# Halvings of modulation sums further apart, and a norm spread moved behind the last head's values

## The chip, the cores and the metric

The kernel runs on one core of one Trainium2 chip. The metric is device time in microseconds (us), as the median of several executions. Beside it there is one profiled execution, whose trace gives the start and length of every instruction on the engines: PE (TensorE, the matrix products), DVE (VectorE), ACT (ScalarE), POOL (GpSimd) and the queue SP that issues most transfers. POOL computes a little here and also issues transfers of its own.

## The reference

One decoder layer on 512 tokens of width 1024, in fp32. Two token mixers run side by side, a gated MLP with a short convolution follows, and everything is modulated by six vectors computed from a condition `c`:

```python
cs = jax.nn.silu(c)
mod = cs @ w_ada[l] + b_ada[l]
shift1, scale1, gate1, shift2, scale2, gate2 = jnp.split(mod, 6, axis=-1)
h = _rmsnorm(x, norm1_g[l]) * (1.0 + scale1) + shift1
proj = h @ w_in[l]
qa, ka, va, qd, kd, vd, ga, gd = jnp.split(proj, points, axis=-1)
out_a = _sliding_window_attention(qa, ka, va, sinks, slopes)      # 8 heads
out_d = _diff_attention(qd, kd, vd, lam, ...)                     # 4 heads, below
merged = sigmoid(ga) * (out_a @ w_branch_swa) + sigmoid(gd) * (out_d @ w_branch_diff)
x = x + gate1 * (merged @ w_out)
h2 = _rmsnorm(x, norm2_g[l]) * (1.0 + scale2) + shift2
x = x + gate2 * _conv_ffn(h2, w_up, conv_w, conv_b, w_down)
```

A differential head takes two causal softmax maps over 64-wide queries and keys, subtracts `lam` times the second from the first, multiplies by 128-wide values, and normalises each token's 128 values by their root mean square (`_rmsnorm(out, subln_g)`). That last norm is what the change touches, together with the sums for `gate1`, `shift2`, `scale2` and `gate2`.

## The kernel before, in words

Every fp32 product is made of three matmuls on a rounded high part and a remainder (`mm3`, lines 129 to 132). The weights arrive in blocks over SP, ACT casts the high part (L126), DVE subtracts for the low part (L127).

The work around the change is the stage of the four differential heads, h = 0 to 3, with four blocks of 128 queries each (n = 0 to 3). TensorE does for each block the scores `sd` (both maps), then, when DVE and ACT have made the softmax and the difference, the transposes `td` (`diff_transpose`), which ACT and DVE evacuate into `aTh` and `aTl` (`evac`, L498 and L499). After the last block of a head come its values: `od` = the transposed maps times the values (`diff_values`). ACT then squares `od` (`sq`) and copies it scaled (`of`).

The norm of a head goes in three closures that `diff_values` leaves behind:

- `stats`: four small matmuls `pss` sum the squares for each token, DVE makes the mean square `ms` (L189), and POOL raises it to the power -1/2 (`rstd_start`, L193);
- `end`: four small DVE operations refine that and multiply in the softmax divisor (`rstd_end`, L201 to L203, and L829): `drs`;
- `turn_norm`: four transposes `rb` (L839) spread `drs` over the partitions, DVE multiplies `of` by it (L841), ACT and DVE split the result into `outdA` and `outdB`, the head's input to the branch product `pB`.

Heads 0 to 2 put these into lists (`beside`) that the main loop empties with `flush` at a fixed block of the next head; head 3 has no next head and uses `after(n, ...)`.

Between these pieces TensorE works off other products, step by step: projections, gates (`pga`, `pgd`) and the branch product of the first mixer (`pA`). `fill(n)` issues n such steps (a step is one `mm3` of 128x512), counts down everything that `after` has put off, and at every eighth step lets the sums of the modulation advance by one step (`ada_rows`).

These sums make four rows of 1024 (`gate1`, `shift2`, `scale2`, `gate2`). DVE multiplies blocks of `w_ada` by `cs` and adds them up in `arow`, 128 partitions by 1024 (L888, L890). The sum over the partitions is done by transfers that POOL issues (`ada_sum`, L898): 64 rows are added onto 64, then 32 onto 32, down to one row, and the last transfer writes it to DRAM (`mod_rows`, L901). Each halving has to wait until the one before it has landed, and POOL, which works in order, stands still meanwhile. `HALVE_LAG` is the number of fills from one halving to the next in the written order.

The readers of `mod_rows`: row 0 becomes `g1b`, by which the output weights are multiplied (L1110, L1118, L1135); rows 1 and 2 are loaded by SP into `m2` (`load_m2`, L1079), turned by TensorE (`turn_m2`, L1083), and scale the second norm; row 3 is read in the MLP. In the trace the tile names have lost their trailing digits: `m2` is `m`, `pm2` is `pm`. `M2_LAG` sets the fills from the end of the attention stage to `load_m2` and to `turn_m2`.

The order of the instructions on TensorE and POOL is the written one (`manual_schedule`); DVE, ACT and SP are ordered by a planner, with priorities (`high_priority`) and with holds (`issue_after`: not before that instruction).

Of the kernel before, what the change touches and what calls it, by code (L numbers as in the profile page):

```python
# [28 lines left out]
ADA_AHEAD = 2  # L29
HP = 100000  # L30
ST = 6
HALVE_LAG = 6
ADA_EVERY = 8
ADA_EASY = 20

ROW_BEHIND = {0: -3, 4: -2}
ADA_START = 4
V_LAG = 13
M2_LAG = (48, 60)
STAT_LAG = 10  # L40
END_LAG = 3
NORM_LAG = 16
# [16 lines left out]
def kernel(  # L59
# [44 lines left out]
    def tbank(name, shape=(P, S)):  # L104
        return bank("t", 2, list(shape), name)

    def vbank(name):
        return bank("v", 1, [P, S], name)
# [16 lines left out]
    def split(hi, lo, src):  # L125
        cast = nc.scalar.copy(hi, src)  # L126
        return cast, nc.vector.tensor_sub(lo, src, hi.bitcast(F32))  # L127

    def mm3(o, lh, ll, rh, rl, start, stop):
        nc.tensor.matmul(o, lh, rh, start=start, stop=False)  # L130
        nc.tensor.matmul(o, lh, rl, start=False, stop=False)  # L131
        nc.tensor.matmul(o, ll, rh, start=False, stop=stop)  # L132
# [53 lines left out]
    def rstd_start(ssq, n, d, wpool, plus=None):  # L186
        ms = wpool.tile([P, n], F32, tag="rs_a", bufs=3, name="ms")
        if plus is None:
            nc.vector.tensor_scalar(ms, ssq, 1.0 / d, EPS, ALU.mult, ALU.add)  # L189
        else:  # L190
            nc.vector.scalar_tensor_tensor(ms, ssq, 1.0 / d, plus, ALU.mult, ALU.add)  # L191
        r0 = wpool.tile([P, n], F32, tag="rs_c", bufs=3, name="r0")
        nc.gpsimd.tensor_tensor(r0, ms, mhalf[:, :n], ALU.pow)  # L193
        return ms, r0

    def rstd_end(dst, ms, r0, n, wpool):
        t = wpool.tile([P, n], F32, tag="rs_b", bufs=3, name="rt")
        if n == 1:
            nc.vector.scalar_tensor_tensor(t, r0, r0, ms, ALU.mult, ALU.mult)
        else:  # L200
            nc.vector.tensor_mul(t, r0, r0)  # L201
            nc.vector.tensor_mul(t, t, ms)
        nc.vector.scalar_tensor_tensor(dst, t, -3.0, r0, ALU.add, ALU.mult)  # L203
# [338 lines left out]
    def prefetch():  # L542
        while units and len(loaded) < 2:
            load, run = units.pop(0)
            loaded.append((load(), run))

    def fill(n):
        for _ in range(n):
            if not current:
                prefetch()  # L550
                if loaded and due[0]:
                    due[0] -= 1
                    wts, run = loaded.pop(0)
                    current.append(run(wts))
                    if tick[0]:
                        prefetch()
            if tick[0] == 7:
                prefetch()
            if current:
                try:  # L560
                    next(current[0])
                except StopIteration:
                    current.clear()
            for e in list(later):
                e[0] -= 1
                if e[0] <= 0:
                    later.remove(e)
                    e[1]()
            tick[0] += 1
            if tick[0] >= ADA_START and tick[0] % ADA_EVERY == 0:  # L570
                next(ada, None)
# [3 lines left out]
    def after(n, fn):  # L575
        later.append([n, fn])

    def flush(*kinds):
        for kind in kinds:
            while beside[kind]:  # L580
                beside[kind].pop(0)()
# [209 lines left out]
    def diff_transpose(s):  # L791
        h, n = divmod(s, NT)
        if n == 0:
            aTs[h] = [ap.tile([P, 1664], F32R, tag=g, bufs=2, name=f"{g}{h}") for g in ("aTh", "aTl")]
        tp = tbank(f"td{h}_{n}")
        for k in range(n + 1):
            nc.tensor.transpose(tp[:, k * P : (k + 1) * P], probs[s][:, k * P : (k + 1) * P], ident)
        hi, lo = (a.rearrange("p (b q) -> p b q", q=P)[:, n : 4 * n + 1 : 3] for a in aTs[h])
        with tc.high_priority(offset=HP):
            settled.append(evac(hi, lo, tp[:, : (n + 1) * P].rearrange("p (k q) -> p k q", q=P)))  # L800

    def diff_values(h):
        t, (aTh, aTl) = heads[h], aTs[h]
        o = vbank(f"od{h}")
        for k in range(NT):
            q0 = k * P
            mm3(
                o[:, q0:], t[:, 4, k * P : (k + 1) * P], t[:, 5, k * P : (k + 1) * P],
                aTh[:, k * AW + q0 : k * AW + 512], aTl[:, k * AW + q0 : k * AW + 512],
                k == 0, k == NT - 1,  # L810
            )
        sq = ap.tile([P, S], F32, tag="tmp", bufs=2, name=f"sq{h}")
        of = ap.tile([P, S], F32, tag="of", bufs=2, name=f"of{h}")
        nc.scalar.activation(sq, o, AF.Square)
        nc.scalar.activation(of, o, AF.Copy, scale=sublnc)

        def stats():
            pss = tbank(f"pss{h}", (P, NT))
            for n in range(NT):
                nc.tensor.matmul(pss[:, n : n + 1], sq[:, n * P : (n + 1) * P], ones[:, 0:1], start=True, stop=True)  # L820
            rs, r0, r2 = (ap.tile([P, NT], F32, tag=t, bufs=2, name=f"{t}{h}") for t in ("drs", "dr0", "dr2"))
            nc.vector.reciprocal(r0, sums[h][:, 0])
            nc.vector.tensor_mul(r2, r0, r0)
            nc.vector.tensor_mul(r2, r2, pss)
            half = rstd_start(r2, NT, P, ap)

            def end():
                rstd_end(rs, *half, NT, ap)
                nc.vector.tensor_mul(rs, rs, r0)  # L829

            if h < 3:
                beside["end"].append(end)
            else:
                after(END_LAG, end)

            def turn_norm():
                rb = tbank(f"rb{h}")
                for n in range(NT):
                    nc.tensor.transpose(rb[:, n * P : (n + 1) * P], rs[:, n : n + 1].to_broadcast([P, P]), ident)  # L839
                with tc.high_priority(offset=HP):  # L840
                    nc.vector.tensor_mul(of, of, rb)  # L841
                split(outd[0][:, h], outd[1][:, h], of)

            if h < 3:
                beside["norm"].append(turn_norm)
            else:
                after(NORM_LAG, turn_norm)

        if h < 3:
            beside["sum"].append(stats)  # L850
        else:
            after(STAT_LAG, stats)
# [42 lines left out]
    def ada_sum(idx, whole):  # L895
        def step(n):
            if n:
                nc.gpsimd.dma_start(whole[0:n], whole[n : 2 * n], accum_op=ALU.add)  # L898
                after(HALVE_LAG, lambda: step(n // 2))
            else:  # L900
                nc.gpsimd.dma_start(mod_rows[idx : idx + 1], whole[0:1].rearrange("o a n -> o (a n)"))  # L901

        after(1, lambda: step(P // 2))
# [98 lines left out]
    for s in range(4 * DIFF_HEADS):  # L1002
        h, n = divmod(s, NT)
        if s in (4, 8):
            due[0] += 3
        elif s == 12:
            due[0] += 4
        ahead = s == 1
        fill(DIFF_FILL[1] - ahead)
        nxt = (s + 1, s + 2) if n % 2 and s < 15 else ()  # L1010
        if nxt:
            diff_scores(*nxt)
        if n == 3:
            with tc.issue_after(maxima[-1].ins):
                flush("end")
        if n == 1:
            diff_transpose(s)
        fill(DIFF_FILL[2] + ahead)
        if n == 2:
            flush("sum")  # L1020
        elif n == 0:
            flush("norm")
        if n != 1:
            diff_transpose(s)
        diff_softmax(*nxt)
        if n == 0 and h:
            diff_values(h - 1)
            fill(DIFF_FILL[3])
    due[0] += 2 * (KT - 4)
    fill(4)  # L1030
    flush("norm")
    diff_values(DIFF_HEADS - 1)
    while due[0] or current:
        fill(1)
    at.close()
# [52 lines left out]

    after(M2_LAG[0], load_m2)
    after(M2_LAG[1], turn_m2)  # L1090

# [880 lines left out]
```

## Time and profile before

| | |
|---|---|
| median of 3 executions | 690.01 us (689.94 to 692.77) |
| the profiled execution | 691.2 us, of which the span from first to last instruction 689.4 us |
| mean granted TensorE clock | 0.994 of full |
| TensorE busy | 677.5 us, 98% of the span |
| DVE, ACT, POOL busy | 563.9, 382.2, 100.1 us |
| halvings on POOL | 28, the first at 135.26, the last at 315.25 us |

A page of the profile lists busy times by engine, then the span in 40 slices with a digit for each engine, then the chain of waits that ended last, then groups of instructions. A row of a timeline has the start, the length, the engine, the line, the operation, its output and inputs, and in brackets how long the engine sat idle before it and what ended that. A row of the chain has start, length and what the time went to. A list of waits has who waited for whom, the total, the number and the longest. A row of the windows has for each engine its busy time and number of instructions, then the granted TensorE clock, the share of the DMA engines and the rate.

### The profile page before, as it was taken

How to read it: one execution, taken by the hardware profiler on the slowest of the kernel's cores; microseconds unless marked ns; L12 is line 12 of the kernel's file. 1: busy time of each engine (PE TensorE's matmuls, PEld its weight loads, DVE VectorE, ACT ScalarE, POOL GpSimd, SP SyncE). 2: the span in 40 equal slices, each digit the busy share in tenths (PEclk: the TensorE clock that was granted, in tenths of full speed). 3: DMA queues.
4: the chain of work that ended last, by engine and by line, in shares of the span. 5: the costliest groups of instructions: out<-in, count | busy, mean ns of one | idle time of the engine just before them, and what ended most of it. 6: DMA issues, size and time to landing. Idle time of an engine off the chain costs nothing.

```text
span 689.4 us, 11101 instructions
## 1 busy us (share of the span) xinstructions
PE 677.5 (98%) x4139; PEld 593.0 (86%) x4139; DVE 563.9 (82%) x1073; ACT 382.2 (55%) x678; POOL 100.1 (15%) x121
## 2 busy tenths in 40 slices
PE   8999999999989999999999999999999999999995
PEld 5887787888878888788899999999999999888885
DVE  5999775988775676793589988888888999979997
ACT  7676674546442323333377656655555666656665
POOL 3000000021012101111030011112110102440300
PEclk9999999999999999999999999999999999999998
DMA  9995412565455687569635788777979647995903
GB/s 306 351 295 180 131 61 76 166 167 157 139 145 160 215 256 201 170 175 327 216 67 119 181 209 191 170 168 216 208 212 220 155 161 182 196 205 144 168 1 122
DMA packets 116934, 123.89 MB, mean 180 GB/s; under 512 B 4983, under 2 KB 93848, under 8 KB 116880
## 3 DMA queue, kind: packets, MB, share of 16 engines
q1 hardware_dynamic: 97038, 95.11, 43.1%
q0 software_dynamic: 19648, 27.79, 23.8%
q8 instruction: 32, 0.52, 0.3%
q10 hardware_dynamic: 194, 0.28, 0.1%
q14 instruction: 22, 0.18, 0.1%
HBM read 118.97 MB, written 2.11 MB: 176 GB/s over the span
## 4 chain that ended last, share of the span: by engine, by line
PE 95%; DMA 2%; DVE 1%; ACT 0%; issue 0%; SPq 0%; POOL 0%; POOLq 0%; ACTq 0%
PE up L1300 32%; PE dc L1916 15%; PE a L393 5%; PE pgd L130 2%; PE pgd L131 2%; PE pgd L132 2%; PE oc L1356 2%; PE oc L1360 2%; PE oc L1357 2%; PE pga L130 2%; PE pga L132 2%; PE pga L131 2%; PE pq L130 1%; PE pw L130 1%; PE sd L137 1%; DMA adaw<-in_w_ada_dram 1%
## 5 line engine op out<-in xcount | busy, mean ns | idle before, releaser
L1300 PE MATMUL up<-t,m_whi 128*128 128x256 f32 x512 | 93.1, 283 | 0.0
L1300 PEld LDWEIGHTS up<-t,m_whi 128*128 128x128 f32 x512 | 79.9, 192 | 0.0
L1300 PE MATMUL up<-t,m_wlo 128*128 128x256 f32 x256 | 72.4, 283 | 0.0
L1300 PE MATMUL up<-bh,p_whi 128*128 128x256 f32 x232 | 65.7, 283 | 0.0
L1300 PE MATMUL up<-bl,p_whi 128*128 128x256 f32 x232 | 65.7, 283 | 0.0
L1300 PE MATMUL up<-bh,p_wlo 128*128 128x256 f32 x232 | 65.7, 283 | 0.0
L898 POOL DMA_DIRECT2D arow<-arow x28 | 22.6, 807 | 254.0 <-DVE sd L783 123.9
L1300 PEld LDWEIGHTS up<-t,m_wlo 128*128 128x128 f32 x256 | 49.2, 192 | 0.0
L1209 POOL DMA_DIRECT2D s<-in_w_up_dram x21 | 26.9, 1354 | 140.9 <-DMA s<-in_w_up_dram 58.9
L1300 PEld LDWEIGHTS up<-bh,p_whi 128*128 128x128 f32 x232 | 44.5, 192 | 0.0
L1300 PEld LDWEIGHTS up<-bl,p_whi 128*128 128x128 f32 x232 | 44.5, 192 | 0.0
L1300 PEld LDWEIGHTS up<-bh,p_wlo 128*128 128x128 f32 x232 | 44.5, 192 | 0.0
L890 DVE SCALAR_TENSOR_TENSOR arow<-ra,cs,arow 128x512 f32<-128x512 f32 x56 | 41.8, 748 | 0.4
L1237 ACT CAST m_whi<-s 128x1024 fp32r<-128x1024 f32 x31 | 32.5, 1049 | 11.1 <-DVE s L1231 6.3
L1241 DVE TENSOR_TENSOR m_wlo<-s,m_whi 128x1024 fp32r<-128x1024 f32 x31 | 37.8, 1219 | 0.0
L1300 PE MATMUL up<-t,p_whi 128*128 128x256 f32 x176 | 32.2, 283 | 0.0
L1300 PEld LDWEIGHTS up<-t,p_whi 128*128 128x128 f32 x176 | 27.5, 192 | 0.0
L1307 ACT ACTIVATE gT<-a,cv 128x512 f32<-128x512 f32 x22 | 17.7, 814 | 16.9 <-DVE a L1342 15.9
L1237 ACT CAST p_whi<-wa 128x1024 fp32r<-128x1024 f32 x18 | 18.8, 1043 | 12.5 <-PE up L1300 12.5
L193 POOL TENSOR_TENSOR r<-ms,mhalf 128x1 f32<-128x1 f32 (+1 forms) x16 | 13.1, 820 | 83.0 <-DVE ms L191 64.8
L1241 DVE TENSOR_TENSOR p_wlo<-wa,p_whi 128x1024 fp32r<-128x1024 f32 x18 | 22.0, 1223 | 3.8 <-ACT p_whi L1237 3.8
L1300 PE MATMUL up<-t,p_wlo 128*128 128x256 f32 x88 | 24.9, 283 | 0.0
(486 smaller groups left out, 2061.6 us busy)
## 6 DMA issues: line engine op xcount, KB each, us to landing
ra<-in_w_ada_dram SPq DMA_DIRECT2D x32, 512.0 KB, 4.3
wa<-in_w_up_dram SPq DMA_DIRECT2D x22, 512.0 KB, 4.6
s<-in_w_up_dram SPq DMA_DIRECT2D x21, 512.0 KB, 5.2
s<-in_w_up_dram POOLq DMA_DIRECT2D x21, 512.0 KB, 7.1
adaw<-in_w_ada_dram SPq DMA_DIRECT2D x12, 512.0 KB, 7.3
w<-in_w_in_dram SPq DMA_DIRECT2D x12, 512.0 KB, 4.9
a<-in_w_up_dram SPq DMA_DIRECT2D x11, 512.0 KB, 4.9
b<-in_w_down_dram SPq DMA_DIRECT2D x10, 512.0 KB, 4.9
```

Of the source, the lines that this page charges most:

```text
L130: nc.tensor.matmul(o, lh, rh, start=start, stop=False)
L131: nc.tensor.matmul(o, lh, rl, start=False, stop=False)
L132: nc.tensor.matmul(o, ll, rh, start=False, stop=stop)
L393: nc.tensor.matmul(acc6[i], lhs[:, i * P : (i + 1) * P], rhs[k], start=k == 0 and p == 0, stop=last and p == 2)
L890: nc.vector.scalar_tensor_tensor(ac, r[:, a], cc, ac, ALU.mult, ALU.add)
L898: nc.gpsimd.dma_start(whole[0:n], whole[n : 2 * n], accum_op=ALU.add)
L1209: nc.gpsimd.dma_start(dst, upblock(*blk), accum_op=ALU.add)
L1237: nc.scalar.copy(W[J, name][0], R[J, SRC[name]])
L1241: nc.vector.tensor_sub(lo, R[J, SRC[name]], hi.bitcast(F32))
L1300: nc.tensor.matmul(o[u], w[:, k, cu], b[:, k], start=name in ("p1", "m5", "p2") and k == 0 and x == 0, stop=k == 3 and x == 2, skip_group_ ...
L1307: nc.scalar.activation(grow(j), av[J][:, u], AF.Identity, bias=cv[:, 66 + j : 67 + j], scale=cv[:, 44 + j : 45 + j])
L1916: nc.tensor.matmul(bank2[u][:, sl], a[:, q, cu], b[:, q, sl], start=first_mm and x == 0, stop=last_mm and x == 2, skip_group_check=name no ...
```

## The change

Four things are edited. The gaps between the seven halvings of a row become 10, 7, 6, 6, 6 and 6 fills instead of 6 each; the write of the row comes 6 fills after the last, as before. `M2_LAG` goes from 48 and 60 to 54 and 66 fills. In the main loop the `end` of head 2 is no longer flushed in the last block (s = 15), where it stood under a hold behind the last maxima, but after the loop, behind 6 fills instead of 4 and without a hold. And the spread of head 2's norm (`turn_norm`) is no longer ahead of the values of head 3, but 8 fills behind them.

```diff
-HALVE_LAG = 6
+HALVE_LAG = (10, 7, 6, 6, 6, 6, 6)
+LAST_NORM = 8
...
-M2_LAG = (48, 60)
+M2_LAG = (54, 66)
...
                 nc.gpsimd.dma_start(whole[0:n], whole[n : 2 * n], accum_op=ALU.add)
-                after(HALVE_LAG, lambda: step(n // 2))
+                after(HALVE_LAG[7 - n.bit_length()], lambda: step(n // 2))
...
-        if n == 3:
+        if n == 3 and nxt:
             with tc.issue_after(maxima[-1].ins):
                 flush("end")
...
     due[0] += 2 * (KT - 4)
-    fill(4)
-    flush("norm")
+    fill(6)
+    flush("end")
     diff_values(DIFF_HEADS - 1)
+    after(LAST_NORM, lambda: flush("norm"))
     while due[0] or current:
         fill(1)
```

## The prediction

> **What bounds the kernel now.** I read the page's busy times first, then TensorE's list of waits, then the chain that ended last around the wait that this list shows, then the instructions of TensorE, POOL and DVE there.
>
> ```profile
> PE 677.5 (98%) x4139; PEld 593.0 (86%) x4139; DVE 563.9 (82%) x1073; ACT 382.2 (55%) x678; POOL 100.1 (15%) x121
> ...
> PE   8999999999989999999999999999999999999995
> PEclk9999999999999999999999999999999999999998
> ...
> PE rb L839 <- DVE drs L829: 1.9, 1, 1.9
> ...
> 195.09 0.65 DVE arow L890
> 196.04 6.76 DMA arow<-arow
> ...
> 203.08 0.78 POOL arow L898
> 203.86 1.07 POOL r L193
> ...
> 206.32 0.71 PE rb L839 x4
> ```
>
> TensorE is busy 98% of the span, so only its own idle time and its clock are to be had. By its list of waits, longest first, its longest wait is `rb` of head 2 (line 839). The chain says why: POOL held a halving (line 898) until the transfer of the halving before it had landed, 6.76 us, and only then did the power for the norm factors (line 193) of head 2, on which `rb` waits. By the page's slices (17.2 us each, in tenths) TensorE is busy without a marked gap behind it, and up to the last slice at full clock: what is saved here should reach the end.
>
> ```profile
> 196.04 0.88 POOL L898 DMA_DIRECT2D arow<-arow  x1 [20.01 <-DVE dr L822]
> 203.08 0.78 POOL L898 DMA_DIRECT2D arow<-arow  x1 [6.16 <-DMA arow<-arow]
> 203.62 1.29 POOL L193 TENSOR_TENSOR r<-ms,mhalf 128x4 f32<-128x4 f32 x1
> ...
> 198.84 0.16 DVE L189 TENSOR_SCALAR ms<-dr 128x4 f32<-128x4 f32 x1
> 204.95 0.16 DVE L201 TENSOR_TENSOR rt<-r 128x4 f32<-128x4 f32 x1 [2.99 <-POOL r L193]
> 205.43 0.68 DVE L499 TENSOR_TENSOR aTl<-td,aTh 128x512 fp32r<-128x512 f32 x1
> ...
> 201.71 0.59 ACT L498 CAST aTh<-td 128x512 fp32r<-128x512 f32 x1 [1.79 <-PE td L797]
> ```
>
> The power's input `ms` is there at 199.0, and POOL begins the power at 203.62: over 4 us late. DVE, in its turn, sits 2.99 us before `rt` (free at 201.96), with the evacuation of the last transposes (`aTl`, input ready at 202.30) queued behind it.
>
> **What the stall costs.** The gap itself, and a slow stretch after it:
>
> ```profile
> 204.06 0.39 PE L132 MATMUL pga<-hThA,wga_l 128*128 128x512 f32 x1
> 206.32 0.71 PE L839 MATMUL rb<-ident,drs 128*128 128x128 f32 x4 [1.87 <-DVE drs L829]
> 206.70 0.76 PE L130 MATMUL od<-aTh,qkv 128*128 128x512 f32 x1
> 210.21 0.44 PE L130 MATMUL pga<-hThA,wga_h 128*128 128x512 f32 x1
> ...
> 182.59 0.39 PE L132 MATMUL pga<-hThA,wga_l 128*128 128x512 f32 x1
> 182.82 0.60 PE L839 MATMUL rb<-ident,drs 128*128 128x128 f32 x4
> 185.23 0.45 PE L130 MATMUL pga<-hThB,wga_h 128*128 128x512 f32 x1
> ...
> 206.50:207.00 0.50, 0.50 (x5) 0.73 0.00 0
> 207.00:207.50 0.50, 0.50 (x3) 0.50 0.00 0
> ...
> 209.50:210.00 0.50, 0.50 (x4) 0.50 0.58 205
> 210.00:210.50 0.50, 0.50 (x5) 0.86 0.91 332
> ```
>
> In the windows the third number after the busy time is the granted clock: 0.50 from about 206.7 to 210.1. Gap: the last `pga` product starts at 204.06, the next instruction would start 0.23 later (182.59 to 182.82), so at 204.29; it starts at 206.32: 2.03 us. Clock: from `rb` to the next `pga` takes 210.21 - 206.32 = 3.89 us here, 185.23 - 182.82 = 2.41 in head 1, where one transpose of `td` lies inside too (a quarter of the 0.38 from 206.32 to 206.70, so 0.1), so 2.31: lost 1.58. Together 3.61 us.
>
> The Trainium skill (TensorE: Matmul & The Clock Gate, Part 1: The HAM clock gate) says that the half clock comes after at least one idle window of about 3.4 us. This trace shows a half clock after 1.87 us idle, so it differs on the idle time; the length of the slow stretch, 3.4 us, agrees with the page's window. Were the page's bound taken at its word, the slow stretch would not be this gap's doing, and the loss would be 2.03 instead of 3.61.
>
> **The change, part by part.** The order on TensorE and POOL is written by hand, and its unit is the fill: one step of a pending product, three matmuls of 0.23 us, 0.69 us together. I counted the fills through the loops. Rows of the modulation are counted from one: row 1 is `mod_rows[0]`.
>
> *Halvings of the second row.* The first (64 rows) comes 8 fills ahead of head 2's `pss` and power. The second comes 6 fills behind the first now, so ahead of the power, as POOL's rows 203.08 and 203.62 show. With 10 it comes 2 fills behind the power. POOL's order is then 64, power, 32, 16, 8: the power starts when `ms` is there, at 199.0, and ends at 200.3 (1.29 us; 1.04 and 1.52 in its rows for other heads, below). The halvings still wait for each other's landing: 32 stays at 203.08. Cost nothing, gain the 4 us of lateness, provided that DVE uses it.
>
> *Rows 1, 3 and 4, and head 3.* The same count for the others:
>
> ```profile
> 149.95 0.81 POOL L898 DMA_DIRECT2D arow<-arow  x1 [2.46 <-DMA arow<-arow]
> 153.31 1.52 POOL L193 TENSOR_TENSOR r<-ms,mhalf 128x4 f32<-128x4 f32 x1 [2.55 <-DVE ms L189]
> ...
> 219.11 1.04 POOL L193 TENSOR_TENSOR r<-ms,mhalf 128x4 f32<-128x4 f32 x1 [3.29 <-DVE ms L189]
> ...
> 226.77 0.52 POOL L901 DMA_DIRECT2D mod_rows<-arow  x1 [1.50 <-DMA arow<-arow]
> 227.30 0.58 POOL L1110 DMA_DIRECT2D g1b<-mod_rows  x1
> ...
> 247.59 0.86 POOL L898 DMA_DIRECT2D arow<-arow  x1 [19.16 <-DVE arow L890]
> 279.69 0.52 POOL L901 DMA_DIRECT2D mod_rows<-arow  x1 [1.52 <-DMA arow<-arow]
> ...
> L1118 DVE TENSOR_TENSOR g1b<-g1b,xn x1: 1220/1220/1220, 241.9 to 241.9; 128x1024 f32<-128x1024 f32 x1
> ```
>
> Row 1: the halving of 8 moves behind head 0's power, which waits for `ms` until 153.31 either way; the row is written behind head 1's power instead of before it, and nobody reads it before 227.30. Row 2: head 3's power now stands behind 8 instead of 4; it waits for DVE in any case (3.29). Halvings 4, 2, 1 come behind it: the row is written some 2 to 3 us later, and with it `g1b` is fetched; `g1b` is used at 241.9, 14.6 after its fetch now. Rows 3 and 4: no power stands between their halvings, and POOL isn't tied to fills otherwise, so nothing moves: 0.
>
> *The end of head 2 and its spread.* `end` (four tiny DVE operations) is written behind the last transposes and two more fills instead of before them, without its hold; `rb` 7 fills behind `od` of head 3 instead of just before it. `od` then starts at 204.29 + 6 x 0.23 = 205.67. It needs `aTl`: input at 202.30, DVE free at 201.96, so done at about 203.0; with `end` ahead of it about 203.7. Margin 2 us. If the planner, freed of the hold, puts `end` right behind `ms`, DVE waits 1.4 us at 199.0 for the power and `aTl` still ends by 204.4: covered. If that cover is gone, `od` waits, which is the second rival. `rb` comes at about 212.4, with `drs` ready since about 204; what hangs on it, head 2's share of the branch product, is first read by `pB` at 252.3. Between `od` and `rb` stand `pga` steps, so TensorE changes over once more. The first `pga` behind such a group shows 0.45 (185.23) where a plain one has 0.39; with one changeover into and one out of it I put 0.1 (bounds 0 and 0.2).
>
> *Second modulation.* The load of rows 2 and 3 (on SP) and its transpose (on TensorE) move by 6 fills, 4.14 us:
>
> ```profile
> L1079 SPq DMA_DIRECT2D m<-mod_rows x1: 331/331/331, 281.3 to 281.3; - x1
> L1083 PEldq EVENT_SEMAPHORE  x1: 51/51/51, 282.9 to 282.9; - x1
> SPq L1079 <- DMA mod_rows<-arow: 8.7, 1, 8.7
> L130 PE MATMUL pB<-outdA,wbd x32: 394/394/394, 252.5 to 307.5; 128*128 128x512 f32 x32
> ```
>
> The transpose has its data at 282.9, as TensorE gets there: no slack today. Afterwards it comes at 283.0 - 3.5 + 4.1 = 283.6. The row's halvings start on DVE work paced by TensorE's products, so they should move 3.5 earlier with it; even unmoved, 0.7 us is left. SP is held 8.7 us for that load today; later in the queue it holds less, and the weights behind it gain. Cost 0.
>
> Sum: -2.03 - 1.58 + 0.1 = -3.5 us. Against the profiled execution's 691.2 (span 689.4) that is 687.7; against the median of the runs, 690.01, it is 686.5. The profiled execution is 1.2 above that median, which could mean that the slow stretch is in it and not in every run.
>
> **Rivals.**
>
> *Only the gap is won.* The slow stretch isn't due to this gap, or isn't in most timed runs. For it: one row alone shows it, and the 1.2 us above. Against: 0.50 begins 0.4 us behind the gap and the page's PEclk, where this stretch still leaves its slice at 9, shows no longer one before the last slice. Gives 690.01 - 2.03 + 0.1 = 688.1.
>
> *The wait moves.* DVE's order is the planner's; if `end` or longer work (a weight's split, a row's step) goes ahead of `aTl`, `od` waits in `rb`'s place. It begins to cost at 2 us late; at 4 us late the gap is as now and the result about 690. Against: `aTl` has high priority. A shorter gap may leave the clock alone, so 689 to 690.
>
> *Slower.* The third row lands late for the transpose. Price: to end 0.5% slower TensorE must lose 3.5 + 3.45 = 7.0 us, 1.6 of it by the clock, so wait 5.4, and the row must land 5.4 + 0.7 = 6.1 us later than now. That gives 693.5. For it: no slack today. Against: the rows' chains, first halving to write, take 30.7 (196.04 to 226.77) and 32.1 us (247.59 to 279.69), 1.4 apart.
>
> **How the numbers follow.** Forecast 0.56 (own range 686.0 to 687.2), only the gap 0.22, moved wait 0.12, slower 0.10. A 0.5% bound, about what a measurement can tell from no change, is 3.45 us, or 686.56; the forecast lies on its edge, and I give it 0.7 of being beyond: faster 0.39. The rest, 0.17 + 0.22 + 0.12 = 0.51, is within; slower 0.10. The range 685.9 to 690.2 takes in all but the slower case and little tails: about 0.15 left out.
>
> **What would show it.** POOL: the power of head 2 at about 199, before the second halving at 203. DVE: no 2.99 us before `rt`, `aTl` by 204. TensorE: no wait on `drs` in its list, `od` at about 205.7, and a granted clock of 1.00 from 206 to 211. SP: a shorter wait of line 1079. Wrong would be: a wait of `od` on `aTl`, a wait of line 1083, or a slow stretch elsewhere.

## The result, and the profile after

The changed kernel takes 688.62 us (median of 20 executions, 687.77 to 690.75), the kernel before in the same series 690.18 (median of 20). The ratio is 0.9973, 95% interval 0.9963 to 0.9983: 1.9 us or 0.27% faster, between 1.2 and 2.6 us; the two medians alone are 1.6 us apart. That lies within 0.5%, in the stated range, and near the rival "only the gap is won" (688.1), not the forecast (686.5). The profiled execution of the changed kernel took 688.92 us with a span of 687.1. The new constant shifts every line number below it by one, and those behind the main loop (the load of the second modulation, the output projection) by two.

POOL's timeline of the changed kernel, where the power of head 2 now stands between the first two halvings:

```profile
196.43 0.83 POOL L899 DMA_DIRECT2D arow<-arow  x1 [19.47 <-DVE dr L823]
199.47 1.03 POOL L194 TENSOR_TENSOR r<-ms,mhalf 128x4 f32<-128x4 f32 x1 [2.22 <-DVE ms L190]
203.21 0.82 POOL L899 DMA_DIRECT2D arow<-arow  x1 [2.71 <-DMA arow<-arow]
```

The power starts when DVE has made `ms`, 4.2 us earlier than before. DVE's timeline shows what becomes of that:

```profile
200.54 0.16 DVE L202 TENSOR_TENSOR rt<-r 128x4 f32<-128x4 f32 x1 [0.59 <-POOL r L194]
...
201.04 1.22 DVE L128 TENSOR_TENSOR wba_l<-wba,wba_h 128x1024 fp32r<-128x1024 f32 x1
...
202.86 0.68 DVE L500 TENSOR_TENSOR aTl<-td,aTh 128x512 fp32r<-128x512 f32 x1
```

The planner put the end of head 2 (`rt` is its first operation) ahead of a weight's split. DVE waits 0.59 us instead of 2.99, and the last evacuation ends at 203.5. TensorE's list of waits and its timeline, then the windows:

```profile
PE xt L417 <- DVE xn L412: 1.8, 2, 1.0
PE a L183 <- POOL ones L142: 1.0, 1, 1.0
PE oc L1359 <- DVE wo_l L128: 0.3, 1, 0.3
...
205.81 0.39 PE L133 MATMUL pga<-hThA,wga_l 128*128 128x512 f32 x1
206.04 0.39 PE L131 MATMUL od<-aTh,qkv 128*128 128x512 f32 x1
...
207.89 0.44 PE L131 MATMUL pga<-hThB,wga_h 128*128 128x512 f32 x1
...
213.40 0.60 PE L840 MATMUL rb<-ident,drs 128*128 128x128 f32 x4
...
206.00:208.00 2.00, 2.00 (x14) 1.00 0.75 215
208.00:211.00 3.00, 3.00 (x15) 1.00 0.93 246
```

The wait of `rb` is gone, `od` follows the last `pga` after the ordinary 0.23 us, and the granted clock stays at 1.00. At this place all that was forecast is there. Matching the same instructions of the two traces, the changed kernel is 0.39 us late up to here, from the start of the program (`xt` waits 1.8 in all instead of 1.3), and 3.3 us early once everything that was moved has been done: the first `pA` behind head 3's spread, at 230.73 before, starts at 227.41. So this pair of traces gives 3.7 us at the place, and the timed executions only half of it. About 1.0 us was given back later in this trace, and 2.3 us are left in the spans: two waits of the output projection `oc` (0.3 for a low part of its weights, 0.2 for its input) are under half of that. The experiments ask whether the trace of before, with its slow stretch, is the ordinary one.

### The profile page after: what moved, and what is told of

Its sections match the earlier page's. It is cut to its first block, busy times and chain, and to the rows that moved or that the text cites. A ratio compares the mean times of both kernels' runs of the same rounds, so it can differ in the third digit from the quotient of the medians.

```text
span 687.1 us, 11101 instructions
## 1 busy us (share of the span) xinstructions
PE 676.2 (98%) x4139; PEld 591.4 (86%) x4139; DVE 564.0 (82%) x1073; ACT 381.2 (55%) x678; POOL 100.1 (15%) x121
## 4 chain that ended last, share of the span: by engine, by line
PE 88%; DMA 7%; issue 2%; DVE 1%; ACT 1%; SPq 0%; POOL 0%; POOLq 0%; ACTq 0%; DVEq 0%
PE up L1302 32%; PE dc L1918 15%; PE a L394 5%; DMA arow<-arow 3%; PE pga L131 2%; PE pga L133 2%; PE pga L132 2%; DMA s_t<-in_w_up_dram 1%; PE sd L138 1%; PE pgd L132 1%; PE pgd L133 1%; PE pgd L131 1%; PE pq L131 1%; DMA adaw<-in_w_ada_dram 1%; PE pw L131 1%
```

## Experiments

The time given as a difference is the ratio to the kernel before in the same series times that kernel's median.

**Keep TensorE busy through the gap.** Eight products that nobody reads, into the bank that `rb` overwrites:

```diff
                 rb = tbank(f"rb{h}")
+                for n in range(8 if h == 2 else 0):
+                    nc.tensor.matmul(rb, hTh[0][:, :P], hTh[0], start=True, stop=True)
                 for n in range(NT):
```

> The kernel before, with eight products of 128x512 issued ahead of the spread of head 2's norm, into the bank that the spread then overwrites. They keep TensorE busy through most of the 2.03 us gap and change no output. Theory (gap and slow stretch are one loss, in every run): no half clock behind the gap, the values of head 3 take 1.95 us instead of 3.5, the time falls by 1.2 to 1.6 us. Rival 1 (the slow stretch is not this gap's doing): the clock still falls to 0.50 for 3.4 us, time unchanged. Rival 2 (the stretch is in the profiled execution only): the profile shows full clock, but the time moves by less than 0.4 us.

Measured: ratio 1.0008 (0.9999 to 1.0017), no gain, as rival 2 had it. The trace (span 688.2) does what was asked:

```profile
204.78 1.98 PE L839 MATMUL rb<-hThA 128*128 128x512 f32 x8
206.59 0.62 PE L841 MATMUL rb<-ident,drs 128*128 128x128 f32 x4
...
208.93 0.44 PE L130 MATMUL pga<-hThA,wga_h 128*128 128x512 f32 x1
...
204.00:206.50 2.50, 2.50 (x13) 1.93 (x11) 1.15 (x6) 0.00 (x0) 1.25 (x2) 1.00 0.93 209
206.50:209.00 2.50, 2.50 (x19) 2.31 (x18) 2.47 (x4) 0.00 (x0) 0.81 (x1) 1.00 0.19 21
```

From `rb` to the next `pga` it is 208.93 - 206.59 = 2.34 us, against 3.89 in the trace of before, and yet no time is won. The eight products themselves add little, since the 1.81 us from the first of them to `rb` (204.78 to 206.59) are no longer than the gap that they fill. So in most timed executions of before the slow stretch wasn't there to be taken away. Their mean clocks say the same. Of 33 executions of the kernel before in this series one has 0.994, like the trace of before, and it is the second longest of them; the others have 0.996 to 0.999.

The mean clock needs care, because in every trace here the clock also falls to 0.50 in the last 2 to 5 us of the program. That end alone leaves a mean of 0.996 (the kernel with only the later load, below) to 0.999 (this trace). The slow stretch takes another 3.4 x 0.5 / 689 = 0.0025. So, with ends like these, 0.994 means that there is a stretch, 0.997 and more mean that there is none, and 0.996 leaves it open.

**A second trace of the kernel before.**

> The kernel before once more, for a second trace of it. In the runs so far 32 of 33 executions of it have a mean clock of 0.996 to 0.999, and the one with 0.994 is among the longest; the trace of before has 0.994. Theory now (the half clock behind the gap is an exception, not the rule): a mean clock of 0.997 or so, the wait of the spread on the norm factors 1.2 to 2.0 us, and full clock behind it. Rival (the stretch is the rule): 0.50 for 3.4 us again.

Its time was 689.63, its span 687.9, its mean clock 0.998. TensorE's waits, timeline and windows:

```profile
PE rb L839 <- DVE drs L829: 1.7, 1, 1.7
...
204.04 0.39 PE L132 MATMUL pga<-hThA,wga_l 128*128 128x512 f32 x1
206.10 0.62 PE L839 MATMUL rb<-ident,drs 128*128 128x128 f32 x4 [1.67 <-DVE drs L829]
...
208.43 0.45 PE L130 MATMUL pga<-hThA,wga_h 128*128 128x512 f32 x1
...
206.00:208.00 2.00, 1.90 (x12) 1.00 0.00 0
208.00:211.00 3.00, 3.00 (x17) 1.00 0.81 207
```

The gap is 206.10 - 204.27 = 1.83 us, and behind it the clock is whole: `rb` to `pga` takes 2.33, the 2.31 of head 1. In this trace there are 1.8 us to be won. Over the four series in which the clocks of before are listed, 2 of 74 executions of it have a mean clock of 0.994, and 12 have the 0.996 that leaves it open. But 0.996 is about as common in the kernels of this document whose gap is gone or filled (11 of 88 executions), so these 12 are no sign of hidden stretches. In the series of the result the clocks of before aren't listed. There 7 of its 20 executions are above 691 us, against 5 of the 74, so for that series the share is open.

**Make the gap longer.** One more small operation of DVE on the factors, which lands behind a step of the sums:

```diff
                 nc.vector.tensor_mul(rs, rs, r0)
+                for _ in range(1 if h == 2 else 0):
+                    nc.vector.tensor_scalar_mul(rs, rs, 1.0)
```

> The kernel before with one more operation of DVE on head 2's norm factors (a product with 1.0), which comes behind one more step of the modulation sums: the spread waits some 0.9 us longer, 2.6 to 2.8 us in all. Theory (the longer the idle time, the more executions get the half clock): most executions at a mean clock of 0.994 to 0.995, and 2.0 to 2.6 us slower than before (0.9 longer wait and 1.6 by the clock). Rival 1 (the half clock comes only with an idle time near 3.4 us): clock 0.997, 0.9 us slower. Rival 2 (chance, whatever the length): a few executions only, 1 us slower.

Measured: ratio 1.0019 (1.0005 to 1.0032), 0.3 to 2.2 us slower and 1.3 in the middle, less than the 2.0 to 2.6 of the theory. The seven executions and their mean clocks, in order:

```
689.61  0.999
689.92  0.997
690.64  0.997
691.59  0.994
691.65  0.994
692.06  0.994
692.94  0.994
```

Four of seven have the clock of the slow stretch and are the four longest. The trace is of one without it, at 2.0 us of waiting (less than I had put, since the power came earlier in that execution):

```profile
PE rb L841 <- DVE drs L831: 2.0, 1, 2.0
...
206.00:208.00 2.00, 1.55 (x10) 1.00 0.07 14
208.00:211.00 3.00, 3.00 (x18) 1.00 0.79 196
```

So with one small operation more in the gap 4 of 7 executions have the low clock instead of 2 of 74, a majority, as the theory had it, and more than the few of rival 2. Those four left no trace: how long they waited, and that their low clock stood at this place, isn't shown. Of the traces, the one with 2.0 us doesn't have the stretch and the one with 1.87 us does, so the length alone doesn't decide, and what else does is open. Against rival 1 stands the trace of before, in which no 3.4 us of idle time were needed.

**One half of the change at a time.** First the halvings and the load only, with `end` and `rb` where they were:

```diff
-HALVE_LAG = 6
+HALVE_LAG = (10, 7, 6, 6, 6, 6, 6)
...
-M2_LAG = (48, 60)
+M2_LAG = (54, 66)
...
-                after(HALVE_LAG, lambda: step(n // 2))
+                after(HALVE_LAG[7 - n.bit_length()], lambda: step(n // 2))
```

> The kernel before with the new gaps of the halvings and the later load of the second modulation (which has to follow the row's write), but the end of head 2 and its spread where they were. Theory (POOL's order alone was the cause): the power at 199.0 to 199.5, the spread at about 204.7 without a wait, full clock, and the time of the changed kernel within 0.5 us: about 688.5. Rival (the new place of the spread is needed): a wait of the spread on the norm factors of 1 us or more remains, and less than half of the changed kernel's gain of 1.6 to 1.9 us is reached.

Its trace has a span of 685.8, among the shortest here, and no wait of `rb`:

```profile
199.16 1.03 POOL L193 TENSOR_TENSOR r<-ms,mhalf 128x4 f32<-128x4 f32 x1 [2.22 <-DVE ms L189]
...
200.23 0.16 DVE L201 TENSOR_TENSOR rt<-r 128x4 f32<-128x4 f32 x1 [0.59 <-POOL r L193]
...
204.36 0.60 PE L839 MATMUL rb<-ident,drs 128*128 128x128 f32 x4
```

But its ratio was 0.9992 (0.9982 to 1.0002), with 5 of 11 executions at 689.3 to 690.5 and the rest at 687.5 to 688.7. The mean clocks of the five are 0.997 to 0.999, so they have no slow stretch. Three runs went after that.

> The kernel with only the halvings and the load moved, once more: five of its eleven timed executions lay 2 to 3 us above the others, and its trace is of a short one. One look has about an even chance to show a long one. Theory: a long one has a wait of the output projection on DVE, with the sum of the up weights issued by POOL at 318 or later. Rival: the wait of the spread of head 2 is back, or the start is longer.

> The same kernel again, for another execution, with the same expectations: a long execution shows a wait of the output projection on DVE (theory), or a wait of the spread of head 2 or a longer start (rival); a short one shows none.

Both were short executions (687.61 and 687.48) without such a wait; they say nothing of the long ones.

> The kernel with only the halvings and the load moved, timed a second time. Its three traces show the whole gain, with no wait behind it, yet 5 of its 11 timed executions were long. Theory (the place of the spread plays no part, and the long ones were chance): ratio to before 0.997 to 0.998, at most 2 of 10 executions above 689.2 us. Rival (with the spread ahead of the values some executions lose 2 to 3 us): ratio 0.999 again, a third to a half of the executions above 689.2 us.

Measured: 687.62, ratio 0.9963 (0.9949 to 0.9976), 687.5 to 688.4 in five executions. The long ones didn't come again in these five. The two series contradict each other beyond their intervals, and what the long executions were is open. They aren't proper to this kernel, since 6 of the 20 executions of the changed kernel in the series of the result are above 689.2 us too. What its four traces and the second series show is that the gain can be had with the spread at its old place.

Then the order only, with the old halvings:

```diff
-        if n == 3:
+        if n == 3 and nxt:
...
-    fill(4)
-    flush("norm")
+    fill(6)
+    flush("end")
     diff_values(DIFF_HEADS - 1)
+    after(8, lambda: flush("norm"))
```

> The kernel before with the old halvings and the old load, but the end of head 2 behind six fills and its spread eight fills behind the values of head 3. DVE's order keeps the end ahead of the last evacuation here. Theory: the power stays at about 203.6 to 204, DVE still waits for it with the evacuation behind it, so the values of head 3 wait on the evacuation from 205.7 to about 206.3, some 0.6 us, too short to bring the half clock: 3.0 of the 3.6 us are won at this place. Rival 1 (the wait moves whole): a wait of 2 us and the half clock, time as before. Rival 2: any idle time brings the half clock: 1.4 won at most.

Measured: 688.16, ratio 0.9976 (0.9967 to 0.9985). POOL's, DVE's and TensorE's timelines:

```profile
203.77 1.30 POOL L193 TENSOR_TENSOR r<-ms,mhalf 128x4 f32<-128x4 f32 x1
...
205.10 0.16 DVE L201 TENSOR_TENSOR rt<-r 128x4 f32<-128x4 f32 x1 [2.51 <-POOL r L193]
205.58 0.68 DVE L499 TENSOR_TENSOR aTl<-td,aTh 128x512 fp32r<-128x512 f32 x1
...
206.29 0.39 PE L130 MATMUL od<-aTh,qkv 128*128 128x512 f32 x1
```

The power is as late as ever, DVE still waits 2.5 us for it, and `aTl` ends at 206.26. With two more fills ahead of it `od` comes at 206.29 and doesn't wait, by 0.03 us: the 0.6 us of waiting that I had put here didn't come, and a landing 0.5 us later, as in the trace of before, would have brought most of it. So each half removes the gap alone: one makes the factors early, the other makes TensorE want them late. Done together they don't add: 1.7 us by this half, 2.6 by the other in its second series (0.6 in its first), 1.8 to 1.9 by both.

**The load of the second modulation.**

```diff
-M2_LAG = (48, 60)
+M2_LAG = (54, 66)
```

> The kernel before with only the load and the turn of the second modulation six fills later. Theory as on record (these edits cost nothing): the time of before within 0.4 us, the output projection without a new wait. Rival (this edit is what costs the changed kernel the 1.1 us that it loses between 309 and 335): waits of the output projection on DVE and 0.5 to 1 us slower than before.

Measured: ratio 0.9998 (0.9990 to 1.0007), which is 0.7 us faster to 0.5 slower. No cost shows, as forecast, and no gain. In its trace, with a mean clock of 0.996, `rb` waits 1.4 us and the granted clock behind it is 1.00 throughout.

**What is given back in the output projection.** In the first trace of the changed kernel the chain of waits leads to the sum of two blocks of the up weights (`s_t`), which stands on POOL behind the halvings of row 4:

```profile
319.49 0.54 issue
320.03 9.82 DMA s_t<-in_w_up_dram
...
329.93 1.06 ACT m5w L127
...
331.02 1.24 DVE m5w L128
...
332.28 1.23 DVE s_t L1233
333.51 1.15 DVE wo_l L128
334.65 0.04 issue
334.70 0.50 PE oc L1359
```

Whether this sum costs the changed kernel time was tried by issuing `s_t` ahead of the last three halvings, which with the row's write now follow it, beside the changed kernel once more:

```diff
         def step(n):
-            if n:
+            if idx == 3 and n == 4:
+                last_row.append(whole)
+            elif n:
...
+    whole = last_row[0]
+    with tc.issue_after(added.ins):
+        for n in (4, 2, 1):
+            nc.gpsimd.dma_start(whole[0:n], whole[n : 2 * n], accum_op=ALU.add)
+        nc.gpsimd.dma_start(mod_rows[3:4], whole[0:1].rearrange("o a n -> o (a n)"))
```

> The changed kernel on the same chip as the two below. Theory: 1.5 to 1.9 us below before, the spread between its executions some 3 us as before, with the long ones held in the output projection by the sum of two blocks of the up weights that stands behind the seventh halving of row 4 on POOL.

> The changed kernel with one transfer moved on POOL: the sum of two blocks of the up weights goes ahead of the last three halvings of row 4 and its write instead of behind the three. Nothing else moves on any engine. Theory (what the changed kernel gives back is the output projection waiting on DVE, which waits on that sum): the sum is issued 8 us earlier, no wait of the output projection on the low part of its weights, the long executions go, the median 0.3 to 1.0 us below the changed kernel and the spread below 2 us. Rival (the giving back has another cause): the time of the changed kernel within 0.2 us.

The changed kernel: 687.94, ratio 0.9974 (0.9963 to 0.9984), 687.3 to 689.0. With `s_t` early: 687.84, ratio 0.9980 (0.9971 to 0.9988), 687.5 to 689.2. The sum was issued at 313.29 instead of 318.19 in the second trace of the changed kernel, 4.9 us earlier and not the 8 expected, and the row's write came at 333.35 instead of 322.78. Neither time nor spread moved. Nor did the second trace of the changed kernel (span 686.4) have the wait of `oc`. Its list of waits, longest first:

```profile
PE a L183 <- POOL ones L142: 1.0, 1, 1.0
PE pc L259 <- POOL ident masks.py:199: 0.2, 1, 0.2
PE a L394 <- ACT hThA L378: 0.2, 1, 0.2
```

No wait is left here but these of the program's first 20 us. Against the second trace of before the `pA` named above starts at 227.40 instead of 228.97, 1.57 us earlier, and the spans differ by 1.5: this pair keeps what it wins. The theory that the changed kernel regularly gives something back in the output projection falls, since the wait is in one of its two traces, and moving the sum gains nothing.

At last the load of the second modulation on POOL's queue, since SP stood still for it:

```diff
-        nc.sync.dma_start(m2[0:16, :], mod_rows[1:3]...)
+        nc.gpsimd.dma_start(m2[0:16, :], mod_rows[1:3]...)
```

> The changed kernel with the load of the second modulation issued by POOL, behind the write of the row, instead of by SP, which holds its queue for 9.2 us waiting for that row with the output weights behind it. Nothing else moves. Theory A (DVE's lateness in the output projection starts at SP's hold): the output weights arrive up to 9 us earlier, the last step of row 4 and with it the sum on POOL come earlier, 0.3 to 1.0 us below the changed kernel. Rival: the weights wait for their buffers anyway, within 0.2 us.

Measured: 687.90, ratio 0.9971 (0.9960 to 0.9982), 687.5 to 688.1 in seven executions. The output weights start at 277.1 instead of 279.5, not 9 us earlier: most of SP's hold is followed by a wait for their buffers. No gain that can be told from the changed kernel.

## Why the prediction was right, and where it was wrong

*The gap, 2.03 us: right.* It is 1.83 in the second trace of before, gone in both traces of the changed kernel, and the measured 1.9 (1.2 to 2.6) needs no other term.

*The clock, 1.58 us: the wrong step.* The sum took the slow stretch of one trace for a part of every execution. It was there in that trace, and with the gap gone no such stretch shows at this place, but only 2 of 74 other executions of before have its mean clock of 0.994, and filling the gap wins nothing. The sign was in the numbers used: the profiled execution was 1.2 us above the median. I named that and gave the case only 0.22 against 0.56; it should have been the forecast. That the time still lies in the stated range is owed to the range, which took in this rival; the sum itself missed by 2.1 us.

In that trace nothing else was idle ahead of the stretch: TensorE is busy 183.96 of the 184 us from 20 to 204. The Trainium skill (TensorE: Matmul & The Clock Gate, Part 1: The HAM clock gate) has the half clock come after at least one idle window of about 3.4 us. As a bound that doesn't hold here, as 1.87 us brought it once; but it points the right way for the forecast, since gaps this short mostly leave the clock alone.

*The changeover, 0.1: nothing.* `od` alone takes 207.89 - 206.04 = 1.85 and `rb` with its follower 0.35 of delay, 2.2 together against the 2.33 of both in company; no cost can be seen, within the bounds given.

*POOL's order and DVE: right.* The power at 199.47 (199.0 plus the 0.39 by which this execution started late), the evacuation by 203.5, `od` at 206.04 (205.67 plus 0.39). The planner did put the end early, and DVE waited 0.6 for it, covered as stated. But the hold had nothing to do with it: the kernel with only the halvings moved keeps the hold and has `rt` just as early (200.23, behind the same 0.59), and the one with only the order changed drops it and has `rt` at 205.10. What moved the end is the earlier power.

*Row 2, 2 to 3 us later: mis-sized, without a price.* It is written at 231.61 instead of 226.77, 4.8 us later. The halvings of 32 and of 16 rows took longer to land: POOL waited 4.72 and 5.38 us behind them instead of 1.84 and 2.40. Why is open. The 14.6 us that I gave to `g1b` after its fetch were not all slack, since DVE now waits for the transfer of the bias `xn` that POOL issues right behind it, at 232.72:

```profile
239.47 1.22 DVE L1120 TENSOR_TENSOR g1b<-g1b,xn 128x1024 f32<-128x1024 f32 x1 [4.98 <-DMA xn<-in_b_ada_dram]
```

So some 7 of the 14.6 us were the transfer's own time. The rest went because DVE came to `g1b` sooner. In both traces its order there is a weight's low part (`wbd`), a step of `arow`, `g1b`; before, it idled 5.08 us for the cast of `wbd`, which is at 231.51 instead of 239.00 in the changed kernel. TensorE isn't seen to wait for `g1b`.

*SP: wrong.* I said that the later load holds SP less. The planner kept it at the same place in SP's queue, behind the same two weights, and the hold is 9.2 us, against 8.7 before (8.6 against 8.9 in the second traces):

```profile
SPq L1081 <- DMA mod_rows<-arow: 9.2, 1, 9.2
```

The transpose didn't wait all the same, and the rival "slower" didn't come.

*What the two halves do.* The part-by-part text took the earlier power and the later `rb` as one means to one end. Either can suffice; I had not said so.

## What to carry to other kernels

Before a stretch of lower clock is put into a sum, hold the profiled execution against the median and look at the mean clocks of other executions: a trace is one execution. A wait can be removed at its source or by moving the waiting instruction behind other work; check whether one of them is enough, as the two didn't add here. The time from a transfer's issue to the use of its data isn't slack: the transfer's own time has to come off, and the use moves forward when what stands ahead of it on its engine is done sooner.

## What was not expected of the hardware

Behind a gap of this length the half clock came in some executions and not in others. A wait of 1.87 us was followed by 3.4 us at 0.50 in one execution, waits of 1.4, 1.7 and 2.0 us in three other traces were not, and with one small operation more in the gap the executions with a mean clock of 0.994 went from 2 of 74 to 4 of 7.
